# The opening norm of a two-layer decoder, computed on a transposed input

## The chip, the cores and the metric

The kernel runs on one core of a Trainium2 chip. The metric is device time in microseconds (us) for one call; smaller is better. Five engines with instruction streams of their own appear in the profile: PE (TensorE, matrix products), DVE (VectorE), ACT (ScalarE), POOL (GpSimd) and SP (SyncE, which here issues nearly all DMA transfers, one after the other in the order of its list).

## The reference

The input x has 1024 tokens of 1024 channels in float32. Two layers follow each other, each with a norm ahead of it; only the first norm and what reads its result, `h`, are touched here.

```python
def rmsnorm(x, g):
    y = x * lax.rsqrt(jnp.mean(x * x, axis=-1, keepdims=True) + NORM_EPS)
    return y * g
...
for i in range(2):                       # layer 0: FoX, layer 1: NSA
    h = rmsnorm(x, norm_g[i])
    x = x + mixer_i(h)                   # the mixer ends with (o * silu(z)) @ w_out
return rmsnorm(x, final_g)
...
def fox_mixer(h, w_in, b_f, w_out):      # layer 0
    q, k, v, f, z = split(h @ w_in)      # 16 heads of 64 channels; f: one gate per head
    c = cumsum(log_sigmoid(f + b_f), axis=tokens)
    logits = q k^T / 8 + c[query] - c[key]          # causal, softmax over the keys
    return (softmax(logits) @ v * silu(z)) @ w_out
```

The norm divides each token by the root of the mean square over its channels and multiplies each channel by a gain.

## The kernel before

TensorE contracts over the 128 partitions, so that every projection of h needs h transposed: channels on partitions, tokens along the free dimension. The names are `P` = 128 partitions, `KC` = 8 chunks of 128 channels, `NT` = 8 tiles of 128 tokens, and two *halves* of 512 tokens. h^T lies in `hT[half]` as two tiles, hi and lo (in the rows `hT0_0_0`, `hT0_0_1` for half 0, `hT0_1_0`, `hT0_1_1` for half 1; the profile calls all of them hT). hi is h rounded to the type fp32r and lo is what the rounding left, h - hi. A weight is split in the same way into `whi` and `wlo` (`load_w`: a 512 KB transfer into `wst`, a cast on DVE, a subtraction on POOL; `wst` has one buffer, `whi` and `wlo` two each). A projection is then three products per chunk, whi with hi, whi with lo, wlo with hi (`mm3`, L132 to L134), 24 products of 512 columns for one half.

**The opening** (`opening`) reads x in eight token tiles of 512 KB and, once, the gain spread over all partitions (`gB`, 512 KB). For each tile, `Norm` squares it on ACT and sums over the channels along the free dimension in the same instruction, ACT takes the root, DVE the reciprocal, and one DVE instruction of 1024 columns (L105) multiplies x by the token's factor and by gB. `to_hT` then transposes: eight products with `ident` into two PSUM tiles (L115), ACT casts them out of PSUM as hi (L119), DVE subtracts for lo (L120). As soon as the first four tiles are through, k_0 (the first half of the k projection of the first pair of heads, from `fox_k(0)`) and pf_0 (the projection to the forget gates, `forget_gate`) are interleaved with the transposes of the last four.

**What is behind it.** `fox_k` evicts each half of k into `KH` and `KL`, ACT and DVE alternating, and copies both across partitions with DMAs. `forget_gate` evicts its projection with two DVE instructions into `f2` and `fT` (L278, L279), passes fT through a DMA that changes its layout (`fg0`), does log-sigmoid and cumulative sum in some twenty short DVE and ACT instructions (L284 to L302), and sums over blocks with one plain float32 product on PE, `pc` (L305). The result goes to DRAM as `cD`, and comes back as the bias tiles `B` (16 transfers of 512 KB over the kernel) to which POOL adds the causal mask (`Bd`, L563). Then follow the projections v (`v_0`, `v_1` for its halves), z and q of the first pair of heads, k, v, q, z of the next ones as fillers between scores, and the attention of the first layer. A helper `wo_copy` writes the output weights back to DRAM in split form in the background (transfers of `wD`), on SP's queue too.

**What sets the order.** In the opening, the lists of PE, DVE and ACT stand in the order of the code (`tc.manual_schedule`); POOL's and SP's lists, and everything behind the opening, are ordered by a scheduler with a model of the costs, which is also free to move instructions that follow in the code. Each engine works its list strictly in order, so an instruction that waits holds up all that stand behind it.

## Time and profile before

| | |
|---|---|
| median of 3 runs | 1571.32 us (1570.53 to 1571.86) |
| profiled execution | 1573.4 us, of which the profile's span is 1571.6 us |
| mean granted TensorE clock in it | 0.98 |
| PE busy | 95% of the span |
| DVE, ACT, POOL busy | 71%, 56%, 35% |
| DMA | 213 MB moved, mean 136 GB/s |

The profile is one execution, and the times are in microseconds from the start of its span. A row of the timeline gives start, duration, engine, line, operation, out<-in and the shapes; in square brackets stands how long the engine was idle before it and what ended that. A row of the page's groups gives, for one line and operation, the count, the busy time and the mean duration in ns, and then the idle time before these instructions. A row of a table by stretches gives, for a window A:B, the busy time and the number of instructions on each engine (PE, its weight loads PEld, DVE, ACT, POOL), then the granted clock, the DMA engines' share and the rate in GB/s. The durations of matmuls are modelled by the profiler and overlap; what counts for them is the distance from start to start. A plain float32 product is two records.

### The profile page before, as it was taken

The numbers are of one execution on the slowest core, as the hardware profiler recorded it, in microseconds if no ns is written. First come the engines' busy times: TensorE is split into PE (matmuls) and PEld (weight loads), VectorE is DVE, ScalarE is ACT, GpSimd is POOL, SyncE is SP. The second block draws the span as 40 slices with busy tenths as digits, with TensorE's granted clock in tenths as the row PEclk, the third lists the DMA queues.
The fourth block names the chain that finished last, engine by engine and source line by source line (L and its number), as shares of the span: only waits on it lengthen the run. The fifth ranks groups of instructions, "written<-read, shape, count | busy, mean of one in ns | idle before, by whom it ended". The sixth has DMA issues, their size and how long they took to land.

```text
span 1571.6 us, 26098 instructions
## 1 busy us (share of the span) xinstructions
PE 1488.9 (95%) x8536; PEld 1245.3 (79%) x8536; DVE 1110.7 (71%) x2880; ACT 873.6 (56%) x2145; POOL 555.6 (35%) x596
## 2 busy tenths in 40 slices
PE   6999999999999787999999989999999999999898
PEld 4888888888777566878888777788888888888786
DVE  6568878788686855456464776888888888887433
ACT  5455655555555643233133544777787788787522
POOL 1222222232223400034242232546555556556400
PEclk9999999999999878999999999999999999999999
DMA  7777787777677756332436555502312312212452
GB/s 259 234 144 163 161 165 150 165 161 160 148 153 171 165 119 208 115 119 90 141 120 186 188 188 174 188 28 82 122 53 69 122 41 68 75 55 81 141 161 94
DMA packets 253945, 213.14 MB, mean 136 GB/s; under 512 B 179632, under 2 KB 201008, under 8 KB 253552
## 3 DMA queue, kind: packets, MB, share of 16 engines
q1 hardware_dynamic: 253808, 211.46, 49.2%
q8 instruction: 68, 1.11, 0.3%
q14 instruction: 69, 0.57, 0.1%
HBM read 123.06 MB, written 46.20 MB: 108 GB/s over the span
## 4 chain that ended last, share of the span: by engine, by line
PE 52%; DVE 12%; ACT 7%; DMA 4%; issue 4%; POOL 1%; SPq 0%; POOLq 0%; DVEq 0%; ACTq 0%
PE ptp_n L1250 7%; PE S_n L1226 7%; PE O_n L1259 3%; PE O_n L1258 3%; PE y L134 3%; PE y L133 3%; PE y L132 3%; ACT cP L1033 2%; DVE hl L594 2%; ACT P L592 1%; PE nz L132 1%; PE nz L133 1%; PE nz L134 1%; DMA wo<-wD 1%; ACT P_n L1234 1%
## 5 line engine op out<-in xcount | busy, mean ns | idle before, releaser
L1238 POOL TENSOR_SCALAR P_n<-P_n,l_n,gates 128x640 f32<-128x640 f32 (+7 forms) x256 | 200.9, 791 | 176.2 <-DVE l_n L1236 143.5
L145 DVE TENSOR_TENSOR ptl_n<-ptp_n,pth_n 128x512 fp32r<-128x512 f32 (+1 forms) x272 | 181.3, 672 | 35.3 <-ACT pth_n L144 31.6
L1234 ACT ACTIVATE P_n<-P_n,m_n 128x640 f32<-128x640 f32 (+7 forms) x256 | 188.5, 737 | 23.8 <-DVE m_n L1233 22.0
L144 ACT CAST pth_n<-ptp_n 128x512 fp32r<-128x512 f32 (+1 forms) x272 | 153.7, 568 | 73.5 <-PE ptp_n L1250 72.1
L592 ACT ACTIVATE P<-P,m 128x512 f32<-128x512 f32 (+1 forms) x192 | 116.8, 609 | 126.6 <-DVE m L583 125.9
L1226 PE MATMUL S_n<-nk,nq 128*128 128x320 f32 (+5 forms) x768 | 171.7, 333 | 0.2 <-DVE m_n L1233 0.2
L1250 PE MATMUL ptp_n<-ident,P_n 128*128 128x128 f32 x1056 | 166.9, 275 | 4.6 <-DVE ptl_n L145 2.9
L563 POOL TENSOR_TENSOR Bd<-B,tri 128x128 f32<-128x128 f32 x128 | 61.4, 491 | 250.6 <-DVE m L583 237.3
L1250 PEld LDWEIGHTS ptp_n<-ident,P_n 128*128 128x128 f32 x1056 | 124.6, 140 | 30.9 <-DVE ptl_n L145 8.1
L1258 PE MATMUL O_n<-pth_n,nv 128*128 128x512 f32 (+3 forms) x384 | 140.1, 369 | 0.8 <-DVE ot_n L1269 0.3
L1226 PEld LDWEIGHTS S_n<-nk,nq 128*128 128x128 f32 x768 | 128.0, 188 | 15.3 <-DVE m_n L1233 1.9
L594 DVE SCALAR_TENSOR_TENSOR hl<-P,hl 128x512 f16<-128x512 f32 (+1 forms) x192 | 125.7, 670 | 19.5 <-ACT hl L593 18.1
L1259 PE MATMUL O_n<-ptl_n,nv 128*128 128x512 f32 (+3 forms) x384 | 120.7, 338 | 0.1
L1233 DVE CUSTOM_DVE_ANT_0 P_n<-S_n,wmask 128x128 f32<-128x128 f32 (+1 forms) x192 | 113.3, 591 | 9.0 <-PE S_n L1226 4.7
L132 PE MATMUL y<-wo,ohi 128*128 128x512 f32 x240 | 97.1, 405 | 8.7 <-ACT ohi L688 4.6
L133 PE MATMUL y<-wo,ohi 128*128 128x512 f32 x240 | 96.6, 403 | 3.7 <-POOL wo L526 3.7
L134 PE MATMUL y<-wo,olo 128*128 128x512 f32 x240 | 95.8, 401 | 2.0 <-DVE olo L468 1.4
L593 ACT ACTIVATE hl<-P 128x512 f16<-128x512 f32 (+1 forms) x192 | 92.7, 513 | 3.4 <-DMA pT<-hl 1.7
L1258 PEld LDWEIGHTS O_n<-pth_n,nv 128*128 128x128 f32 x384 | 72.6, 189 | 6.9 <-DVE ot_n L1269 1.3
L574 PE MATMUL S<-KH,Q 128*128 128x512 f32 (+1 forms) x192 | 68.7, 372 | 8.0 <-DVE m L583 7.8
L1259 PEld LDWEIGHTS O_n<-ptl_n,nv 128*128 128x128 f32 x384 | 73.0, 190 | 2.2 <-DVE ptl_n L145 0.3
L608 PE MATMUL O<-v,pT 128*128 128x128 f16 x576 | 61.8, 226 | 8.3 <-DVE ot L620 4.7
(361 smaller groups left out, 4030.1 us busy)
## 6 DMA issues: line engine op xcount, KB each, us to landing
nq<-qD SPq DMA_DIRECT2D x64, 256.0 KB
B<-cD SPq DMA_DIRECT2D x16, 512.0 KB
wo<-wD SPq DMA_DIRECT2D x16, 512.0 KB
nq<-qD SPq DMA_DIRECT2D x64, 128.0 KB
of<-oF SPq DMA_DIRECT2D x12, 512.0 KB
x<-in_x_dram SPq DMA_DIRECT2D x8, 512.0 KB
wst_k<-in_fox_w_dram SPq DMA_DIRECT2D x8, 512.0 KB
wst_v<-in_fox_w_dram SPq DMA_DIRECT2D x8, 512.0 KB
```

What stands on the lines that cost most here:

```text
L132: T.matmul(ps, wh, mh, start=first, stop=False, **kw)
L133: T.matmul(ps, wh, ml, start=False, stop=False, **kw)
L134: T.matmul(ps, wl, mh, start=False, stop=last, **kw)
L144: A.copy(hi[:, 0:n], pt[:, 0:n])
L145: V.tensor_tensor(lo[:, 0:n], pt[:, 0:n], f(hi[:, 0:n]), OP.subtract)
L594: V.scalar_tensor_tensor(lo[:, cs], L[:, 0:n], UP, hi[:, cs], OP.mult, OP.subtract)
L1226: T.matmul(ps[:, b, 0:w], self.q[x][:, qi * P:(qi + 1) * P], k[:, k0 + b * w:k0 + b * w + w], start=(x == 0), stop=(x == 1))
L1234: A.activation(L, L, AF.Exp, bias=m, scale=-1.0, accum_out=lr[:, 0, qi:qi + 1])
L1238: G.tensor_scalar(L, L, lr[:, 1, qi:qi + 1], gates[:, i, x:x + 1], OP.mult, OP.mult)
L1250: T.transpose(pt[:, (x + i) * P:(x + i + 1) * P], L[:, kb * P - k0:(kb + 1) * P - k0], ident)
L1258: T.matmul(po[:, d], v, hi[:, c], start=(b == i == 0), stop=False)
L1259: T.matmul(po[:, d], v, lo[:, c], start=False, stop=(b == len(self.blocks) - 1 and i == len(pieces) - 1))
```

## The change

x is passed a second time in transposed layout, `xT`, and the gain as `norm_gT`, one column of 128 for each chunk. Only the opening of layer 0 uses them; x itself is still read later for the residual. In the opening, channels are now on partitions from the start:

- x^T is loaded in 16 pieces of 256 KB (128 channels by 512 tokens); gB is no longer loaded.
- ACT squares a piece into `sq` (two buffers), and PE sums over the channels: four plain float32 products per piece, each with 128 tokens of sq as the stationary side and a column of ones as the moving side, accumulating over the eight chunks in PSUM (`sum_0`, `sum_1`, one column per token tile).
- `factors(half)`: root on ACT, reciprocal on DVE, a DVE copy that repeats each token's factor along 128 columns (`rb`), and four plain float32 products of it with ident, which leave in PSUM a tile (`r_0`, `r_1`) with each token's factor on all partitions.
- `chunk(half, k, eng)`: one DVE instruction multiplies the piece by the gain and by that tile (L373), ACT casts the result to hi (L375), and lo is subtracted on DVE for even and on POOL for odd chunks (L376).
- The transposes and their evictions are gone. k_0 is interleaved with the chunks of half 0 and the sums of half 1, pf_0 and the second half of k with the chunks of half 1.

```diff
     def opening():
-        gB = st.tile([P, D], F32, name="gB")
-        xs = []
-        for t in range(NT):
-            xs.append(st.tile([P, D], F32, tag="x", bufs=7, name=f"x_{t}"))
-            dma(xs[t], a["x"][t * P:(t + 1) * P, :])
-            if t == 0:
-                dma(gB, a["norm_g"][0:1, :].to_broadcast([P, D]))
-            if t == 1:
-                wst = wp.tile([P, KC, P], F32, tag="wst", bufs=1, name="wst_k0")
-                dma(wst, a["fox_w"][8])
-            if t == 3:
-                dma(wfst, a["fox_w_f"].rearrange("(k p) c -> p k c", p=P))
-                dma(bf, a["fox_b_f"].rearrange("o h -> h o"))
-                dma(below, a["below"])
+        gT = st.tile([P, KC], F32, name="gT")
+        dma(gT, a["norm_gT"])
+        wst = wp.tile([P, KC, P], F32, tag="wst", bufs=1, name="wst_k0")
+        xs = [st.tile([P, KC, 512], F32, name=f"xT_{half}") for half in range(2)]
+
+        def load_x(half, ks):
+            for k in ks:
+                dma(xs[half][:, k, :], a["xT"][k * P:(k + 1) * P, half * 512:half * 512 + 512])
+
+        load_x(0, range(6))
+        dma(wst, a["fox_w"][8])
+        load_x(0, range(6, 8))
+        dma(wfst, a["fox_w_f"].rearrange("(k p) c -> p k c", p=P))
+        dma(bf, a["fox_b_f"].rearrange("o h -> h o"))
+        dma(below, a["below"])
+        load_x(1, range(8))
         dma(tri, a["tri"])
+        ones = st.tile([P, 1], F32, name="ones")
+        G.memset(ones, 1.0)
         whi = wp.tile([P, KC, P], F32R, tag="whi", bufs=2, name="whi_k0")
         wlo = wp.tile([P, KC, P], F32R, tag="wlo", bufs=2, name="wlo_k0")
-        side = []
-        hs = {}
+        sums = [ps_s(f"sum_{half}") for half in range(2)]
+        rs = [ps_s("r_0"), ps_t("r_1")]
+
+        def square(half, k):
+            sq = st.tile([P, 512], F32, tag="sq", bufs=2, name=f"sq_{half}_{k}")
+            A.activation(sq, xs[half][:, k, :], AF.Square)
+            for t in range(4):
+                T.matmul(sums[half][:, t:t + 1], sq[:, t * P:(t + 1) * P], ones, start=(k == t == 0), stop=(k == KC - 1 and t == 3))
+
+        def factors(half):
+            r = st.tile([P, 8], F32, name=f"rms_{half}")
+            A.activation(r[:, 0:4], sums[half][:, 0:4], AF.Sqrt, bias=eps, scale=1.0 / D)
+            V.reciprocal(r[:, 4:8], r[:, 0:4])
+            rb = st.tile([P, 4, P], F32, name=f"rb_{half}")
+            V.tensor_copy(rb, r[:, 4:8, None].to_broadcast([P, 4, P]))
+            for t in range(4):
+                T.matmul(rs[half][:, t * P:(t + 1) * P], rb[:, t, :], ident, start=(t == 0), stop=(t == 3))
+
+        def chunk(half, k, eng):
+            h = st.tile([P, 512], F32, tag="h", bufs=3, name=f"h_{half}_{k}")
+            V.scalar_tensor_tensor(h, xs[half][:, k, :], gT[:, k:k + 1], rs[half], OP.mult, OP.mult)
+            hi, lo = (hT[half][i][:, k, :] for i in range(2))
+            A.copy(hi, h)
+            eng.tensor_tensor(lo, h, f(hi), OP.subtract)
+
         with tc.manual_schedule(engines={T.engine, V.engine, A.engine}):
-            for t in range(NT + 1):
-                if t < NT:
-                    nm = Norm(st, xs[t], f"n0_{t}", 3)
-                    nm.square(slice(0, D))
-                    hs[t] = nm.finish(gB)
-                if t:
-                    to_hT(hs.pop(t - 1), t - 1, hT, f"n0_{t - 1}", (ps_s, ps_t))
-                if t == 1:
-                    V.tensor_copy(whi, wst)
-                    G.tensor_tensor(wlo, wst, f(whi), OP.subtract)
-                    wq.append((whi, wlo))
-                if t == 4:
-                    V.tensor_copy(wf[:, :, 0:H], wfst)
-                    V.tensor_tensor(wf[:, :, 32:32 + H], wfst, f(wf[:, :, 0:H]), OP.subtract)
-                    side = [k0] * 9 + [gate0] * 8
-                if t >= 5:
-                    for g in side[0:5]:
-                        next(g)
-                    del side[0:5]
-            for g in side:
-                next(g)
+            for k in range(KC):
+                square(0, k)
+            V.tensor_copy(whi, wst)
+            G.tensor_tensor(wlo, wst, f(whi), OP.subtract)
+            wq.append((whi, wlo))
+            factors(0)
+            for k in range(KC):
+                chunk(0, k, V if k % 2 == 0 else G)
+                square(1, k)
+                if k:
+                    next(k0)
+            V.tensor_copy(wf[:, :, 0:H], wfst)
+            V.tensor_tensor(wf[:, :, 32:32 + H], wfst, f(wf[:, :, 0:H]), OP.subtract)
+            factors(1)
+            next(k0)
+            next(k0)
+            side = [gate0] * 8 + [k0] * 8
+            for k in range(KC):
+                chunk(1, k, V if k % 2 == 0 else G)
+                for g in side[0:2]:
+                    next(g)
+                del side[0:2]
...
     r["x"] = np.ascontiguousarray(inputs["x"][0])
+    r["xT"] = np.ascontiguousarray(r["x"].T)
+    r["norm_gT"] = np.ascontiguousarray(inputs["norm_g"][0].reshape(KC, P).T)
```

Behind the opening the code is unchanged, but the scheduler's lists move. Three places show it. The first is PE's list around the first product of k_0. Before (transposes `pth`, the x4 of a row are four products):

```order
L115 MATMUL pth_n0_3_0_205<-ident_72,h_n0_3_180 128x128 x4
L115 MATMUL pth_n0_3_1_212<-ident_72,h_n0_3_180 128x128 x4
L115 MATMUL pth_n0_4_0_227<-ident_72,h_n0_4_200 128x128 x4
L115 MATMUL pth_n0_4_1_234<-ident_72,h_n0_4_200 128x128 x4
L132 MATMUL k0_0_245<-hT0_0_0_94,whi_k0_127 128x512
L133 MATMUL k0_0_245<-hT0_0_1_95,whi_k0_127 128x512
L134 MATMUL k0_0_245<-hT0_0_0_94,wlo_k0_128 128x512
L132 MATMUL k0_0_245<-hT0_0_0_94,whi_k0_127 128x512
```

Now (`sum_0`, `sum_1` are the sums of squares, `r_0` the spread factors):

```order
L360 MATMUL sum_0_133<-ones_129,sq_0_6_175 128x1 x4
L360 MATMUL sum_0_133<-ones_129,sq_0_7_181 128x1 x4
L369 MATMUL r_0_135<-ident_72,rb_0_192 128x128 x4
L360 MATMUL sum_1_134<-ones_129,sq_1_0_202 128x1 x4
L360 MATMUL sum_1_134<-ones_129,sq_1_1_212 128x1 x4
L132 MATMUL k0_0_222<-hT0_0_0_94,whi_k0_131 128x512
L133 MATMUL k0_0_222<-hT0_0_1_95,whi_k0_131 128x512
L134 MATMUL k0_0_222<-hT0_0_0_94,wlo_k0_132 128x512
L360 MATMUL sum_1_134<-ones_129,sq_1_2_230 128x1 x4
```

What moved: the transposes are gone, and ahead of k_0's first product now stand all sums of half 0, the factors and the sums of two pieces of half 1; one group of sums stands between each two chunks of k_0.

The second place is DVE's list in the second half, from the eviction of k_0 on. Before (`KL_0_0` and `KL_0_1` are evictions of k_0, `f2` and `fT` those of the gate's projection `pf_0`, the outputs hT0_1_1 the lo tiles of half 1):

```order
L324 TENSOR_TENSOR KL_0_0_243<-k0_0_245,KH_0_0_241 64x512
L324 TENSOR_TENSOR KL_0_1_244<-k0_0_245,KH_0_1_242 64x512
L101 RECIPROCAL st_n0_7_303<-st_n0_7_303 128x1
L105 SCALAR_TENSOR_TENSOR h_n0_7_304<-x_7_124,st_n0_7_303,gB_103 128x1024
L120 TENSOR_TENSOR hT0_1_1_97<-pth_n0_6_0_309,hT0_1_0_96 128x4x128
L120 TENSOR_TENSOR hT0_1_1_97<-pth_n0_6_1_316,hT0_1_0_96 128x4x128
L120 TENSOR_TENSOR hT0_1_1_97<-pth_n0_7_0_333,hT0_1_0_96 128x4x128
L120 TENSOR_TENSOR hT0_1_1_97<-pth_n0_7_1_340,hT0_1_0_96 128x4x128
L278 COPY f2_299<-pf_0_300 16x512
L279 SCALAR_TENSOR_TENSOR fT_298<-pf_0_300,bf_99,f2_299 16x512
```

Now:

```order
L324 TENSOR_TENSOR KL_0_0_220<-k0_0_222,KH_0_0_218 64x512
L324 TENSOR_TENSOR KL_0_1_221<-k0_0_222,KH_0_1_219 64x512
L373 SCALAR_TENSOR_TENSOR h_1_0_326<-xT_1_107,gT_103,r_1_136 128x512
L278 COPY f2_331<-pf_0_332 16x512
L376 TENSOR_TENSOR hT0_1_1_97<-h_1_0_326,hT0_1_0_96 128x512
L373 SCALAR_TENSOR_TENSOR h_1_1_337<-xT_1_107,gT_103,r_1_136 128x512
L373 SCALAR_TENSOR_TENSOR h_1_2_345<-xT_1_107,gT_103,r_1_136 128x512
L279 SCALAR_TENSOR_TENSOR fT_330<-pf_0_332,bf_99,f2_331 16x512
L376 TENSOR_TENSOR hT0_1_1_97<-h_1_2_345,hT0_1_0_96 128x512
L373 SCALAR_TENSOR_TENSOR h_1_3_353<-xT_1_107,gT_103,r_1_136 128x512
```

What moved: the eviction f2 of pf_0, which stood behind the last of the lo subtractions of the second half, now stands behind the first chunk's product h_1_0 and ahead of its lo subtraction, and fT ahead of the lo of the third chunk.

The third place is POOL's list in the opening (`wlo_k0`, `wlo_v0` are split weights, L128 and L382 the same subtraction). Before:

```order
L361 TENSOR_TENSOR wlo_k0_128<-wst_k0_109,whi_k0_127 128x1024
L128 TENSOR_TENSOR wlo_v0_434<-wst_v0_431,whi_v0_433 128x1024
L128 TENSOR_TENSOR wlo_q0_440<-wst_q0_437,whi_q0_439 128x1024
L128 TENSOR_TENSOR wlo_z0_527<-wst_z0_524,whi_z0_526 128x1024
L563 TENSOR_TENSOR Bd_0_0_0_1_607<-B_0_0_602,tri_74 128x128
```

Now:

```order
L382 TENSOR_TENSOR wlo_k0_132<-wst_k0_105,whi_k0_131 128x1024
L376 TENSOR_TENSOR hT0_0_1_95<-h_0_1_208,hT0_0_0_94 128x512
L376 TENSOR_TENSOR hT0_0_1_95<-h_0_3_239,hT0_0_0_94 128x512
L128 TENSOR_TENSOR wlo_v0_460<-wst_v0_457,whi_v0_459 128x1024
L376 TENSOR_TENSOR hT0_0_1_95<-h_0_5_265,hT0_0_0_94 128x512
L376 TENSOR_TENSOR hT0_0_1_95<-h_0_7_291,hT0_0_0_94 128x512
L376 TENSOR_TENSOR hT0_1_1_97<-h_1_1_337,hT0_1_0_96 128x512
L376 TENSOR_TENSOR hT0_1_1_97<-h_1_3_353,hT0_1_0_96 128x512
```

What moved: eight lo subtractions of 512 columns are new on POOL, and the subtraction for v's weight stands in the middle of the four of half 0. On DVE, likewise, the cast of z's weight (`whi_z0`) stood behind the forget gate's arithmetic and now stands behind its second instruction (L284, L293). From v_1 on, PE's two lists are the same up to the place of the single product pc. On SP's list, twelve of the wD copies now stand ahead of the second half's KH and KL transfers and of the gate's layout transfer.

## The prediction

> **What bounds the kernel now.** I read the page for the whole, a table by stretches for the opening, then the timeline of the first 75 us engine by engine, and last the groups of instructions for prices.
>
> ```profile
> PE 1488.9 (95%) x8536; PEld 1245.3 (79%) x8536; DVE 1110.7 (71%) x2880; ACT 873.6 (56%) x2145; POOL 555.6 (35%) x596
> core 0: us, PE busy (x) PEld busy (x) DVE busy (x) ACT busy (x) POOL busy (x), PEclk, DMA share, GB/s
> 0.00:23.70 23.70, 9.37 (x39) 7.78 (x40) 14.89 (x21) 14.55 (x29) 3.75 (x9) 1.00 0.89 321
> 23.70:39.00 15.30, 13.96 (x71) 11.36 (x70) 11.38 (x19) 8.00 (x16) 3.38 (x1) 1.00 0.49 169
> 39.00:60.00 21.00, 21.00 (x94) 17.25 (x94) 10.49 (x25) 6.91 (x12) 3.28 (x2) 1.00 0.85 280
> 60.00:100.00 40.00, 40.00 (x196) 33.08 (x195) 24.43 (x59) 18.40 (x40) 13.90 (x14) 1.00 0.54 143
> ```
>
> TensorE bounds all but the opening: from 39 to 100 us it never stops. So the change is worth the shift of one point on PE, behind which nothing is new. I take the start of v_1, the second half of the first v projection: from there PE runs the same list before and after, but for the one product pc. These rows fix the points before:
>
> ```profile
> 23.82 0.78 PE L132 MATMUL k<-hT,whi_k 128*128 128x512 f32 x1
> ...
> 31.02 0.40 PE L275 MATMUL pf<-hT,wf 128*128 128x512 f32 x1
> ...
> 52.61 0.39 PE L134 MATMUL v<-hT,wlo_v 128*128 128x512 f32 x1
> 52.83 0.39 PE L132 MATMUL v<-hT,whi_v 128*128 128x512 f32 x1
> ```
>
> The first projection, k_0, starts at 23.8 and has its last product finished at about 31.2; v_1 starts at 52.8. Warm, a 512-column product takes 0.2275 us of PE (start to start), so three are 0.68.
>
> **Price of a sum.** The sums are plain f32, and PE writes a plain f32 product as two records, each with a weight load. The only such product before is pc:
>
> ```profile
> 58.28 0.28 PE L305 MATMUL pc<-fg,below 128*128 128x1 f32 x2
> 58.42 0.48 PE L132 MATMUL q<-hT,whi_q 128*128 128x512 f32 x1
> 58.73 0.39 PE L133 MATMUL q<-hT,whi_q 128*128 128x512 f32 x1
> ...
> 22.20 1.97 PE L115 MATMUL pth_n<-ident,h_n 128*128 128x128 f32 x8 [0.98 <-DVE h_n L105]
> ...
> 28.06 1.03 PE L115 MATMUL pth_n<-ident,h_n 128*128 128x128 f32 x8
> ```
>
> From 58.28 to 58.73 stand both halves of pc and one 512-column product: 0.45 - 0.23 = 0.22, so 0.11 per record, though it streams one column: the load is what it pays for. A chunk (four tokens' tiles, two records each) is 8 x 0.115 = 0.92 us. That is with a fast PE. Eight transposes take 1.97 us at 22.2 and 1.03 at 28.1: early on PE runs at half speed, and a chunk is then about 1.8. When it gets fast is seen here:
>
> ```profile
> 25.25 0.48 PE L132 MATMUL k<-hT,whi_k 128*128 128x512 f32 x1
> 25.57 0.39 PE L133 MATMUL k<-hT,whi_k 128*128 128x512 f32 x1
> ...
> 22.05:25.46 3.41, 3.26 (x12) 2.97 (x13) 3.34 (x8) 2.97 (x6) 0.00 (x0) 1.00 0.00 0
> 568.20:571.60 3.40, 1.82 (x7) 0.89 (x6) 3.37 (x15) 2.23 (x6) 0.92 (x2) 1.00 0.50 96
> 571.60:575.00 3.40, 2.98 (x22) 2.43 (x22) 1.61 (x9) 2.05 (x7) 0.00 (x0) 0.50 0.31 63
> 581.80:585.20 3.40, 3.40 (x10) 2.63 (x9) 1.74 (x6) 0.71 (x2) 0.00 (x0) 0.50 0.43 84
> ```
>
> PE got fast at 25.4, after 3.2 us with almost no gap; at 568 to 571.6 it was busy for 1.82 of 3.40 us and slow afterwards; 2.98 of 3.40 did not bring it back, an unbroken stretch did. [...]
>
> **First half, k_0.** The first chunk lands about when x lands now (ACT's first Square starts at 4.58). Prices of the rest:
>
> ```profile
> L525 ACT CAST wo<-wo 128x512 fp32r<-128x512 f32 x32 | 18.2, 617 | 11.2 <-DMA wo<-wD 10.8
> L100 ACT ACTIVATE st_n<-st_n,eps 128x1 f32<-128x1 f32 x8 | 2.4, 294 | 0.3
> L632 DVE SCALAR_TENSOR_TENSOR z<-pto,vsc,z 128x512 f32<-128x512 f32 x16 | 12.0, 747 | 18.1 <-PE pto L630 17.9
> L901 DVE TENSOR_TENSOR rt_q<-rt_q,ru_q 128x512 f32<-128x512 f32 x4 | 2.6, 680 | 0.0
> L1275 POOL TENSOR_TENSOR no<-no,nz 128x512 f32<-128x512 f32 x16 | 21.1, 1320 | 4.1 <-DVE nz L82 3.3
> L324 DVE TENSOR_TENSOR KL<-k,KH 64x512 fp32r<-64x512 f32 x4 | 2.8, 688 | 2.6 <-ACT KH L323 2.5
> L323 ACT CAST KH<-k 64x512 fp32r<-64x512 f32 x4 | 2.3, 582 | 8.8 <-PE k L134 7.3 <-DVE KL L324 1.5
> ...
> 13.18 2.35 POOL L361 TENSOR_TENSOR wlo_k<-wst_k,whi_k 128x1024 fp32r<-128x1024 f32 x1 [11.19 <-DVE st_n L101]
> 13.21 3.40 DVE L105 SCALAR_TENSOR_TENSOR h_n<-x,st_n,gB 128x1024 f32<-128x1024 f32 x1
> ```
>
> - Sums of half 0: first Square done at 5.2; two chunks on a slow PE (3.6), six on a fast one (5.7), 0.2 to drain: 14.7. The loads hide below this: eight 256 KB pieces and the 512 KB weight at 1251.00's rate (last fence) land by about 11.
> - Factors: Sqrt 0.29, reciprocal 0.16, spreading copy between 0.35 and 0.68 (half a 1024-column weight cast at one end, a 512-column copy out of PSUM at the other; I take 0.5), eight records with 128 columns 1.0 and draining 0.25: 17.1 with hand-overs. Then h 0.75 and its cast 0.62: 18.5.
> - Sums 0 and 1 of half 1 stand ahead of k_0's first product on PE; their Square comes behind that cast (19.1). PE has been three quarters idle since 15 and is slow: 3.6 more. k_0 starts at 22.7, no earlier than now by more than a microsecond.
> - The loop then has two limits of the same size. PE: 0.92 + 0.68 + 0.09 for a weight load with nothing over it = 1.7 per chunk. DVE with POOL: the 1024-column product of DVE at 13.21 took 3.40 us where its equals take 1.28, exactly because POOL subtracts until 15.53; both have two inputs in SBUF. The odd chunks' subtractions on POOL therefore shut out the even ones' on DVE: h 0.72, cast 0.62, POOL 1.33, DVE 0.62 and hand-overs 0.1 in a row make 3.4 per two chunks, 1.7 per chunk. Eight chunks: 13.6. Half a slow product at the start and POOL's wlo_v (2.35), now in the middle of the loop between DVE's cast and its next subtraction, add 1 to 2.5, taken as 1.6. k_0 finishes at 37.9 against 31.2: 6.7 late. Bounds: 34 if PE is fast throughout and wlo_v hides; 41.
>
> **Second half, to v_1.** KH, KL, KH, KL alternate on ACT and DVE: 2.7. h_0 0.7. Then DVE's list has f2, which waits for the sixteen pf products (3.7, end at 37.9 + 3.9 = 41.8); f2 0.68, subtraction 0.65: 43.1. Three pairs at 3.4: 53.3. The last chunk, h 0.65, cast 0.65, POOL 1.35: 56.0. Its five products 1.15 and the 17 of v_0 that stand behind them 3.9: v_1 starts at 61.1, 23.2 after k_0. Before it was 21.6 (31.2 to 52.8), transposes included. So 1.6 more, bounds -1.5 (no shutting out: three pairs at 2.3) and +2.5. PE fills the waits with seven products of v_0, no more.
>
> **Behind v_1.** DVE's cast whi_z now stands ahead of the forget gate's arithmetic, and it waits for the last product that reads whi_v:
>
> ```profile
> 58.30 0.69 DVE L127 CAST whi_z<-wst_z 128x1024 fp32r<-128x1024 f32 x1 [0.26 <-PE v L133]
> ...
> 71.39 1.72 POOL L563 TENSOR_TENSOR Bd<-B,tri 128x128 f32<-128x128 f32 x4 [9.87 <-DMA B<-cD]
> 1251.00:1251.50 0.50, 0.50 (x5) 0.45 (x4) 0.44 (x2) 0.44 (x2) 0.00 (x0) 1.00 0.90 320
> ```
>
> The gate's chain behind it takes 5 us (table load 1.28, Ln and some twelve short DVE instructions), PE reaches pc 4.3 us after v_1's end: 0.7 of waiting. The bias B, which now comes just as the first scores do (71.39 against 71.0), comes some 3 us late; PE has 75 products of z and k before the next scores, so I cost it at 0 to 2.8, taking 0.5. Removed and costing nothing: gB's 512 KB, the PSUM evictions, 64 transposes (13 us of PE busy time, all of it in waits for DVE). On SP, twelve of the wD copies now go ahead of the second KH and of fg's load; at 1.4 us each they are through by 54, fg comes at 60. If they are not, fg adds to those 2.8.
>
> **Sum.** 6.7 + 1.6 + 0.7 + 0.5 = 9.5 us later. The profiled execution took 1573.4 (span 1571.6), 2.1 above the median of 1571.3; so 1582.9 in a profile like it, 1580.8 as the median.
>
> **Rivals.**
> - *PE stays slow through the sums.* If only streamed columns make PE fast, one-column products never do. Half 0: 5.2 + 8 x 1.8 = 19.6; factors on a slow PE 3.8, h and cast 1.4: 24.8; then eight times (1.8 + 1.43), the second spreading 2: 53. Plus 23.2: 76, and with the tail +24.5: 1596. Against it: at 22.05 to 25.46 1.97 us were transposes, and PE still came up, while 2.98 us of mostly long products at 571.6 did not suffice: occupied time seems to count. [...] Chance 0.22.
> - *DVE and POOL don't shut each other out, or sums are nearly free.* Without the first, half 2 saves 3.2 and half 1 about 1: +5.3, 1576.6; with both, k_0 at 31 to 32 and 1572. The 3.40 us row is against it. Chance 0.1.
> - *Given back behind (not slower).* From 540 to 630 us PE is busy for 72 of 90 us. If a wait there ended on a transfer that does not depend on the opening, 9 us would vanish: 1571 to 1573. It decides if the oF and pT transfers there start at the same time as before; they carry products of the first layer, which come late. Chance 0.1.
>
> [...] Here slow transposes take 0.25 each, fast ones 0.13; no one-column product on a slow PE is shown.
>
> **Chances.** My case 0.58 (own range 1577 to 1586), the rivals 0.22, 0.1, 0.1. The range to hold 8 in 10: 1573 (low prices) to 1597 (slow PE). A change under 0.2% (3.1 us) can't be told from none: faster 0.04, same 0.11 (given back, lowest prices), slower 0.85.
>
> **What would show it.** First k product near 22.7, last near 37.9; sum chunks at 1.8 and then 0.92; subtractions on POOL at 1.3 and DVE's with a mean well over 0.68; v_1 at about 61; the rest shifted alike. I am wrong if k_0 ends by 31 (sums or exclusion overpriced) or after 50 (slow PE).

## The result, and the profile after

The changed kernel takes 1594.45 us (median of 4 runs, 1593.84 to 1596.46) against 1571.59 (1570.53 to 1572.40) for the kernel before on the same chip: a ratio of 1.0148 [1.0131, 1.0166], 22.9 us slower. The sign was forecast; the size, 9.5 us, was less than half of it. The time lies within the range given, but at the place of the rival in which PE stays slow through the sums (1596). The profiled execution took 1596.46 us, 2.0 above its median, as the profiled execution of before was 1.8 above this one.

The page of after, its first line, and the table by stretches over the first three stretches shown for before:

```profile
PE 1516.3 (95%) x8616; PEld 1271.5 (80%) x8616; DVE 1107.8 (69%) x2876; ACT 873.4 (55%) x2139; POOL 566.2 (36%) x605
0.00:23.70 23.70, 15.86 (x72) 15.51 (x72) 2.05 (x4) 7.41 (x13) 3.80 (x10) 1.00 0.87 299
23.70:39.00 15.30, 14.55 (x56) 13.31 (x56) 9.06 (x14) 7.91 (x15) 7.50 (x5) 1.00 0.30 106
39.00:60.00 21.00, 19.01 (x67) 15.38 (x67) 7.62 (x12) 3.91 (x7) 1.99 (x2) 0.97 0.44 150
```

PE's share is still 95% and its busy time has *grown* by 27 us, though 64 transposes are gone. It is now PE that is busy from 5 us on, and DVE, busy for 14.89 of the first 23.7 us before, is nearly idle (2.05). The granted clock reads 1.00 in the first two rows; nothing in this column says that PE is slow, and the last section tells why. The timeline of PE says it:

```profile
5.32 13.79 PE L360 MATMUL sum<-ones,sq 128*128 128x1 f32 x64 [5.32 <-ACT sq L358]
20.19 2.08 PE L369 MATMUL r<-ident,rb 128*128 128x128 f32 x8 [1.09 <-DVE rb L367]
...
28.05 0.77 PE L132 MATMUL k<-hT,whi_k 128*128 128x512 f32 x1
28.62 0.63 PE L133 MATMUL k<-hT,whi_k 128*128 128x512 f32 x1
29.05 0.63 PE L134 MATMUL k<-hT,wlo_k 128*128 128x512 f32 x1
29.48 1.70 PE L360 MATMUL sum<-ones,sq 128*128 128x1 f32 x8
31.04 0.78 PE L132 MATMUL k<-hT,whi_k 128*128 128x512 f32 x1
...
44.41 1.70 PE L360 MATMUL sum<-ones,sq 128*128 128x1 f32 x8
...
47.40 1.91 PE L369 MATMUL r<-ident,rb 128*128 128x128 f32 x8
...
51.66 0.56 PE L276 MATMUL pf<-hT,wf 128*128 128x512 f32 x1
52.06 0.39 PE L275 MATMUL pf<-hT,wf 128*128 128x512 f32 x1
...
73.83 0.39 PE L132 MATMUL v<-hT,whi_v 128*128 128x512 f32 x1
84.98 0.38 PE L305 MATMUL pc<-fg,below 128*128 128x1 f32 x2 [1.47 <-DVE fg L301]
93.74 0.48 PE L602 MATMUL S<-KH,Q 128*128 128x512 f32 x1
```

The first row holds all sums of half 0: 64 records without a gap in 13.79 us, 0.215 each, and not one of the eight groups gets shorter. ACT, which has two sq buffers, waits for PE instead (idle 1.07 ahead of each Square from the third on). In the loop a chunk takes 2.99 us (28.05 to 31.04): 1.56 for its sums and 1.43 for three long products, the last two 0.43 apart, where on a fast PE they are 0.23 apart. PE is busy without a gap from 28 to 50 and remains at this speed (0.43 between long products). The last sums end at 45.97. Then come three long products (of 512 columns), the spreading of half 1 and only long products, and PE gets fast at 52: the pf products are 0.23 apart from there. It is slow once more (0.43) from 58.8 to 62.3, around three waits of 0.91, 0.46 and 0.63 us for chunks of half 1. k_0 ends at about 50.6, v_1 starts 21.0 us later than before, the first score product S 22.7 later, and the span ends 23.1 later. Nothing is given back behind the opening.

### The profile page after: what moved, and what is told of

Its sections match the earlier page's. It is cut to its first block, busy times and chain, and to the rows that moved or that the text cites. A ratio compares the mean times of both kernels' runs of the same rounds, so it can differ in the third digit from the quotient of the medians.

```text
span 1594.7 us, 26274 instructions
## 1 busy us (share of the span) xinstructions
PE 1516.3 (95%) x8616; PEld 1271.5 (80%) x8616; DVE 1107.8 (69%) x2876; ACT 873.4 (55%) x2139; POOL 566.2 (36%) x605
## 4 chain that ended last, share of the span: by engine, by line
PE 68%; DVE 14%; ACT 7%; issue 4%; DMA 4%; POOL 1%; SPq 0%; POOLq 0%; DVEq 0%; ACTq 0%
PE ptp_n L1278 6%; PE S_n L1254 6%; PE O_n L1287 3%; PE y L134 3%; PE y L133 3%; PE O_n L1286 3%; PE y L132 3%; DVE hl L622 2%; PE k L132 2%; PE k L133 2%; PE v L132 2%; PE k L134 2%; PE v L133 2%; PE v L134 2%; ACT P L620 2%
## 5 line engine op out<-in xcount | busy, mean ns | idle before, releaser
L1262 ACT ACTIVATE P_n<-P_n,m_n 128x640 f32<-128x640 f32 (+7 forms) x256 | 188.5, 738 | 25.4 <-DVE m_n L1261 23.7
L636 PEld LDWEIGHTS <-pT 128*128 128x128 f16 x576 | 50.8, 100 | 22.8 <-issue 15.4
```

The source lines that it names most:

```text
L1262: A.activation(L, L, AF.Exp, bias=m, scale=-1.0, accum_out=lr[:, 0, qi:qi + 1])
```

## The experiments

Each expectation has a theory A and a theory B of its own. Theory A of e1, e2 and e7 is that only streamed columns make PE fast, so that one-column products never do. The times below are from the start of each profiled span. Three points on PE's list for every kernel, and the median with its ratio to before:

| kernel | last k_0 product | v_1 | first S | median us | ratio to before |
|---|---|---|---|---|---|
| before | 30.79 | 52.83 | 71.00 | | |
| after | 49.96 | 73.83 | 93.74 | 1594.45 | 1.0148 [1.0131, 1.0166] |
| e1_stream | 39.02 | 61.64 | 81.61 | 1584.76 | 1.0083 [1.0065, 1.0101] |
| e2_block | 46.41 | 69.26 | 91.60 | 1595.90 | 1.0150 [1.0134, 1.0165] |
| e3_lo_dve | 50.02 | 71.03 | 91.36 | 1595.50 | 1.0147 [1.0132, 1.0162] |
| e4_acc | 40.85 | 61.40 | 83.58 | 1584.43 | 1.0077 [1.0060, 1.0094] |
| e6_f32r | 38.68 | 58.67 | 79.14 | 1579.63 | 1.0051 [1.0035, 1.0066] |
| e7_feed | 36.10 | 56.06 | 76.53 | 1579.48 | 1.0043 [1.0030, 1.0056] |
| e9_pc | 50.16 | 72.80 | 90.70 | 1591.54 | 1.0123 [1.0108, 1.0138] |
| e8_order | 34.90 | 55.59 | 75.43 | 1577.65 | 1.0027 [1.0016, 1.0038] |
| e10_psum | 32.99 | 52.12 | 73.77 | 1573.53 | 1.0008 [0.9993, 1.0024] |
| e11_gate | 32.97 | * | 72.10 | 1573.13 | 0.9999 [0.9988, 1.0010] |
| e12_gate2 | 32.16 | * | 69.67 | 1572.63 | 1.0000 [0.9989, 1.0012] |
| e13_gate3 | 31.72 | * | 65.90 | 1567.70 | 0.9958 [0.9944, 0.9971] |

(* v_1 is interleaved with other work there. Each ratio is to the runs of before on the same chip, whose medians were 1571.6 to 1573.5.) From S to the end of the span there remain 1496.8 to 1501.4 us in all of them. So the opening decides, but a difference of up to 4.6 us between two kernels can also arise behind it.

### Is it the columns? e1_stream

The same squares, still plain f32, become the moving side: 512 streamed columns against a stationary block of ones.

```diff
-            for t in range(4):
-                T.matmul(sums[half][:, t:t + 1], sq[:, t * P:(t + 1) * P], ones, ...)
+            T.matmul(sums[half], ones, sq, start=(k == 0), stop=(k == KC - 1))
```

The sums come out along the free dimension; eight tiny records bring the roots back onto partitions.

> Sums by one plain float32 product per piece in which the squares are the moving side (512 columns, ones as 128x128 stationary side), the same kind of product and on a slow PE about the same PE time per piece (1.7 us) as the four one-column products; the row of sums is then turned back into a column by four small products, 1 to 2 us more per half. Theory A (only streamed columns make PE fast, one-column products leave it slow): the first two to four pieces take 1.7 us each, then 0.9; sums of half 0 done at 14 to 16 us instead of 19.1, first k product at 22 to 24 instead of 28.05, last at about 37 to 40 instead of 50, whole time 1581 to 1585 against 1594.5. Theory B (plain float32 products never make PE fast, or PE is slow here for another reason, such as the time since the start): 1.7 us per piece throughout, first k product at 29 to 30, last at about 51, time 1595 to 1597.

The timeline of PE in e1_stream:

```profile
5.37 9.82 PE L359 MATMUL sum<-sq,ones 128*128 128x512 f32 x16 [5.37 <-ACT sq L358]
...
24.11 1.41 PE L132 MATMUL k<-hT,whi_k 128*128 128x512 f32 x1
...
26.08 1.02 PE L359 MATMUL sum<-sq,ones 128*128 128x512 f32 x2
...
27.64 1.02 PE L359 MATMUL sum<-sq,ones 128*128 128x512 f32 x2
...
39.02 0.40 PE L134 MATMUL k<-hT,wlo_k 128*128 128x512 f32 x1
```

PE gets fast within the sums of half 0, whose 16 records take 9.82 us, and which are done at 15.2 instead of 19.1; the spreading behind them takes 1.16, where after needed 2.08. It falls slow again behind the factors (the four records from 20.99 take 3.12, 0.78 each), and is fast from the second chunk of k_0 on. In the loop a chunk takes 1.56 us (26.08 to 27.64); three fast products take 0.69 of them, which leaves 0.87 for the two records, near the 0.92 at which the prediction had priced the one-column ones. k_0's last product comes 10.9 us earlier and the median is 9.7 us lower. All of it is as theory A had it, the first k product 0.1 us later. It also agrees with the sum of the main case, whose premise was a fast PE: k_0 ends at 39.4 (forecast 37.9), and the kernel is 12.4 us slower than before on its chip (forecast 9.5).

### Long products alone: e2_block

The sums of half 1 all go ahead of k_0, so that its 24 products stand together.

```diff
             for k in range(KC):
                 chunk(0, k, ...)
                 square(1, k)
-                if k:
-                    next(k0)
...
+            for k in range(KC):
+                next(k0)
```

> As the changed kernel, but all sums of half 1 stand ahead of k_0's first product on PE instead of between its chunks; the number of products is the same. Theory A (the one-column products between the chunks keep PE slow): the sums still take 1.7 us per group, the first k product comes at 36 to 38 us, and then 24 products without sums between them get fast after 3.4 to 7 us, so that k_0 ends at about 45 to 46 instead of 50.6 and the whole time falls by 4 to 6 us to about 1589. Theory B (PE is slow until about 52 us whatever stands between the products): k products 0.43 us apart to the end, k_0 ends at 47 to 48, PE fast no earlier than 51, time about 1592.

The timeline of PE in e2_block, at k_0 and behind the wait at pc:

```profile
39.32 0.77 PE L132 MATMUL k<-hT,whi_k 128*128 128x512 f32 x1
...
42.45 0.63 PE L133 MATMUL k<-hT,whi_k 128*128 128x512 f32 x1
...
43.23 0.40 PE L132 MATMUL k<-hT,whi_k 128*128 128x512 f32 x1
...
79.67 0.38 PE L305 MATMUL pc<-fg,below 128*128 128x1 f32 x2 [2.08 <-DVE fg L301]
...
80.70 0.63 PE L132 MATMUL q<-hT,whi_q 128*128 128x512 f32 x1
```

PE gets fast in the middle of k_0, 3.9 us behind its first product (0.43 apart up to 42.88, 0.23 from 43.23 on); behind the sums ahead of it, 10.4 us of one-column products in one unbroken row (0.217 each), it was still slow. The last k_0 product comes 3.6 us earlier, much as theory A expected. The total was a miss: v_1 came 4.6 earlier, S only 2.1. PE waited longer at pc (2.08 us against 1.47) and fell slow again behind it (0.43 apart from 80.70 to 83.69). The median did not move by more than its uncertainty, where theory A had 4 to 6 us.

### The shutting out of DVE and POOL: e3_lo_dve

All subtractions for lo go to DVE, each one chunk behind its h.

```diff
-            eng.tensor_tensor(lo, h, f(hi), OP.subtract)
+            return lambda: V.tensor_tensor(lo, h, f(hi), OP.subtract)
...
+                nxt = chunk(half, k + 1, V) if k < KC - 1 else None
+                lo()
+                lo = nxt
```

> As the changed kernel, but all lo subtractions are on DVE, each behind the next chunk's product h. First half bounded by PE's sums, so k_0 ends at 50 to 51 as before. Theory A (a POOL subtraction shuts out the DVE subtraction with both inputs in SBUF): the stretch from k_0's end to v_1 shrinks from 23.2 to about 20.5 us, DVE's subtractions have a mean of 0.65 instead of about 1.0, time about 1592. Theory B (POOL takes work off DVE, no exclusion): the stretch stays at 23 or grows by up to 2 us, time 1594 to 1597.

The groups by line, DVE's and POOL's subtractions, first in after, then in e3_lo_dve:

```profile
L376 DVE TENSOR_TENSOR hT<-h,hT 128x512 fp32r<-128x512 f32 x8 | 7.7, 968 | 6.5 <-ACT hT L375 6.5
L376 POOL TENSOR_TENSOR hT<-h,hT 128x512 fp32r<-128x512 f32 x8 | 10.6, 1326 | 41.0 <-ACT hT L375 41.0
```

```profile
L376 DVE TENSOR_TENSOR hT<-h,hT 128x512 fp32r<-128x512 f32 x16 | 11.6, 722 | 3.1 <-ACT hT L375 3.1
```

With POOL's share taken over, DVE's subtractions get *shorter*, from a mean of 968 ns to 722. From k_0's end to v_1 pass 20.4 us instead of 23.2, as expected; how much of that is the shorter subtractions and how much the other order on DVE's list, the run doesn't separate. In the loop of half 0 nothing is gained, since there PE is the limit. The median did not show the 2.4 us by which S came earlier; its uncertainty is as large.

### Fewer sums on PE: e4_acc

DVE adds up the squares of the eight pieces, and PE sums once per half. lo as in e3.

```diff
+            V.tensor_tensor(acc[half], acc[half], sq, OP.add)
...
+        def total(half):
+            for t in range(4):
+                T.matmul(sums[half][:, t:t + 1], acc[half][:, t * P:(t + 1) * P], ones, ...)
```

> The squares are added up over the chunks on DVE (seven additions of 512 columns per half), so that PE does four one-column products per half instead of 32; lo on DVE as in the run beside it; the weight k is loaded behind all pieces of half 0 and its lo subtracted on DVE. Theory A (what the change lost is the 128 slow records of sums and the slow k products between them): r_0 is there at about 15 to 16 us, first k product at 17.5 to 19, the first half is then bounded by DVE (h, lo and an addition, 2.0 us per chunk), k_0 ends at 32 to 35, v_1 starts at 52 to 56 against 73.8 and 52.8 before the change; time 1571 to 1575. Theory B (the loss is in the order of half 2 or behind v_1, not in the sums): at most 10 us of the 23 come back, time 1584 or more.

The timeline of PE in e4_acc, and its row in the table by stretches:

```profile
30.01 0.79 PE L133 MATMUL k<-hT,whi_k 128*128 128x512 f32 x1 [2.42 <-DVE hT L383]
...
35.74 1.87 PE L367 MATMUL sum<-ones,acc 128*128 128x1 f32 x8 [2.65 <-DVE acc L363]
20.00:41.00 21.00, 13.79 (x32) 8.65 (x33) 16.21 (x26) 7.93 (x15) 2.84 (x1) 1.00 0.71 266
```

A miss: k_0 starts at 20.2, 3.6 us earlier than before, but its last product comes at 40.85 and not by 35. PE is busy for 13.8 of 21 us and waits for DVE, which now adds, multiplies and subtracts for every chunk (16.2 of 21 us), once 2.42 while POOL's wlo_v holds up DVE's subtraction (2.18 us, the others 0.68), and 2.65 for the last sum of half 1. With these gaps PE stays slow too (0.43 between products up to 40.2). The load moved from PE to DVE, and half of the loss is back. The time, 1584.43, is what theory B had (1584 or more), but not for its reason: v_1 comes 12.4 us earlier than in after.

### Sums in fp32r, and a PE kept busy: e6_f32r, e7_feed

e6 streams the squares as in e1, but rounded to fp32r (one record instead of two), with lo on DVE, the weight of k behind all pieces of half 0, and the factors of half 1 ahead of k_0's last chunk. e7 is e6 with 34 products of a zero weight, whose result is overwritten, put ahead of and among the sums of half 0.

```diff
-            sq = st.tile([P, 512], F32, ...)
+            sq = st.tile([P, 512], F32R, ...)
...
+        def feed(n):            # only in e7: feed(12) first, feed(2) behind each piece, feed(6)
+            for i in range(n):
+                T.matmul(rs[1], wf[:, 0, :], wf[:, 0:4, :], start=True, stop=True)
```

> Sums as in e1_stream, but with the squares rounded to fp32r (one product of 512 columns per piece, 0.23 to 0.43 us of PE instead of 0.9 to 1.7); all lo subtractions on DVE one chunk behind h, as in e3_lo_dve; the weight k behind all pieces of half 0, its lo on DVE; factors of half 1 ahead of k_0's last chunk, and the first two h of half 1 ahead of k_0's eviction. Theory A (what the change lost is the slow one-column products on PE and then the sharing of DVE with POOL; the transposed opening by itself needs less of PE and DVE than the one before): r_0 at 16 to 18 us, first k product at 18 to 20, last at 29 to 32, v_1 at 46 to 50 against 52.8 before the change, first scores at 65 to 70 against 71.0, time 1565 to 1571. Theory B (the transposed opening is slower in itself, by its factors and DVE's two passes over h): v_1 at 55 or later, time over 1574.

> As e6_f32r, with 34 more products of 512 columns on PE whose operands are zeros and whose result is overwritten, from about 2 us until r_0: they do nothing but keep PE streaming. Theory A (streaming alone makes PE fast): dummy products 0.43 us apart at first, 0.23 from 5 to 9 us on; the small products that turn the sums into a column take 0.11 instead of 0.21 us per record and the spreading 1.0 instead of 2.0 us, r_0 comes 1 to 2 us earlier than in e6_f32r and v_1 0 to 2 us earlier. Theory B (PE is slow early for another reason, or zeros do not count): no product under 0.4 us before 15 us, and the added products only delay.

The timeline of PE in e6_f32r, then in e7_feed:

```profile
13.83 1.86 PE L367 MATMUL r<-one,row 1*128 1x1 f32 x8 [0.83 <-ACT row L365]
16.43 2.08 PE L372 MATMUL r<-ident,rb 128*128 128x128 f32 x8 [0.74 <-DVE rb L370]
```

```profile
2.05 5.49 PE L364 MATMUL r<-wf 128*128 128x512 f32 x12 [2.05 <-POOL wf L266]
...
8.40 0.40 PE L360 MATMUL sum<-sq,ones 128*128 128x512 f32 x1
...
13.78 1.05 PE L371 MATMUL r<-one,row 1*128 1x1 f32 x8 [0.36 <-ACT row L369]
15.57 1.16 PE L376 MATMUL r<-ident,rb 128*128 128x128 f32 x8 [0.74 <-DVE rb L374]
```

With streamed columns of zeros PE gets fast as well: it is so from about 8 us on, after 6 us of them (0.43 from product to product at 7.33, 0.23 at 8.40), and the tiny records and the spreading then cost 1.05 and 1.16 instead of 1.86 and 2.08. So in these runs the slow PE of the first 25 us is no matter of elapsed time, but of what PE has been given to do. v_1 comes 2.6 us earlier in e7 than in e6, though PE falls slow twice more, from about 21.8 and from about 32 us (0.43 apart from 21.93 to 24.91 and from 35.67 to 38.66); the medians are equal within their uncertainty. By its numbers e6 is theory B's case (v_1 at 58.67 and 1579.63 us, where theory A had 46 to 50 and 1565 to 1571). That the transposed opening is slower in itself does not follow: e10 below brings v_1 ahead of before's with another order. What is left in e6 is DVE, which stands idle for 4.54 and 1.57 us around the factors of half 1: its reciprocal waits for the tiny records, which stand behind seven chunks of k_0 on PE's list.

### The wait at pc: e9_pc

The kernel after, with pc reading a zero instead of the gate's last scan: the sums over blocks are left out of the cumulative sum.

```diff
-        T.matmul(pt[:, 0:1], below, r[:, 3:4], start=True, stop=True)
+        T.matmul(pt[:, 0:1], below, zero, start=True, stop=True)
```

> As the changed kernel, but the product pc reads a constant column of zeros instead of the forget gate's block sums (that part of the cumulative sum is left out), so that PE does not wait for DVE there. Theory A (of the 23 us, 1.5 to 1.8 lie behind v_1, in PE's wait at pc, as DVE's cast whi_z delays the gate's arithmetic): from v_1 to the first scores 18.2 to 18.6 us instead of 19.9, time 1.3 to 1.8 us shorter. Theory B (the first scores wait for the bias B or for q anyway): still 19.5 to 20, no difference.

PE's list now has pc at 54 us, ahead of v_1, and no wait there. From v_1 to S pass 17.9 us instead of 19.9, a little more than theory A expected, and the median is 2.9 lower (1591.54 against 1594.45; the intervals of the two ratios still touch). So the gate's chain on DVE, which stands behind the cast whi_z, costs the changed kernel about 2 us, where the prediction had 0.7 and 0.5 for the bias behind it.

### Can the change be repaired? e8_order, e10_psum, e11_gate, e12_gate2, e13_gate3

All are e7 with another order. e8 squares six pieces of half 1 ahead of k_0, takes the factors of half 1 behind the fourth chunk of k_0, and interleaves pf_0 with it. e10 also splits `factors` in two, so that DVE need not wait in the middle, spreads the squares of half 1 over the first chunks of half 0, and gives pf_0 another PSUM tile.

```diff
 # e8 against e7
+            for k in range(6):
+                square(1, k)
+                feed(1)
...
+                if k == 3:
+                    factors(1)
 # e10 against e8
-            pt = ps_a(f"pf_{half}")
+            pt = (ps_a if half else ps_s)(f"pf_{half}")
...
+                if k == 3:
+                    column(1)
+                if k == 4:
+                    spread(1)
```

> As e7_feed (sums streamed in fp32r, PE kept streaming until r_0, lo on DVE), with another order: squares and sums of half 1 right behind the factors of half 0, so that the factors of half 1 are there before DVE is through with half 0; pf_0 interleaved with k_0 and pf_1 with the second half of k. In e6_f32r DVE stood idle for 4.5 and 1.6 us around the factors of half 1 and ACT and PE had idle time from 14 to 19 us. Theory A (e6_f32r and e7_feed were held by this order, not by what the transposed opening needs): DVE works without a gap over 1 us from the first h at about 17 to the last lo at about 43, v_1 at 46 to 49 us against 56.1 and 52.8 before the change, first scores at 65 to 69 against 71.0, time 1565 to 1570. Theory B (the wait at pc and the gate's chain, not the opening, set the first scores): v_1 early, but PE's wait at pc grows by as much, first scores at 71 to 76, time 1571 or more.

> As e8_order, with its three gaps mended: pf_0 is accumulated in a PSUM tile of the scores' pool, so that pf_1 needs no tile that DVE has yet to clear (PE stood still for 4 us there, and was slow for 3 more); the squares of half 1 are spread over the first three chunks of half 0 instead of ahead of them (ACT's casts, and so DVE, waited 2.2 us); the reciprocal of half 1 stands one chunk later on DVE than the root on ACT (DVE waited 2.5 us). Theory A (these gaps held e8_order): DVE's last lo at 43 to 45 us instead of 48.6, v_1 at 48 to 51 instead of 55.6, first scores at 68 to 71 against 71.0 before the change, time 1569 to 1573. Theory B (DVE is full anyway, or other waits take their place): v_1 at 53 or later, time 1574 or more.

e8 missed what was expected of it: v_1 comes at 55.6, not at 46 to 49. k_0 is through by 35.3, but then PE stops for DVE's subtraction and falls slow (0.43 apart from 40.80 on), as its timeline shows; below it the timeline of e10_psum at pc and its table by stretches:

```profile
40.06 0.51 PE L133 MATMUL k<-hT,whi_k 128*128 128x512 f32 x1 [2.88 <-DVE hT L383]
40.40 0.60 PE L134 MATMUL k<-hT,wlo_k 128*128 128x512 f32 x1
```

```profile
62.50 0.38 PE L305 MATMUL pc<-fg,below 128*128 128x1 f32 x2 [1.61 <-DVE fg L301]
59.00:62.50 3.50, 1.90 (x9) 1.24 (x7) 2.24 (x12) 2.35 (x5) 1.83 (x1) 1.00 0.56 215
64.00:67.00 3.00, 3.00 (x8) 2.33 (x8) 0.42 (x3) 0.51 (x1) 0.00 (x0) 0.50 0.88 151
```

In e10 v_1 starts at 52.1, 0.7 earlier than before: the opening's loss is gone. But PE is half idle ahead of pc and slow from 64 to 67 (8 products in 3 us), and S comes 2.8 us later than before. Both are a little later than theory A had them (48 to 51, and 68 to 71). The time ties with before, since 3.8 us less remain behind S. e11 and e12 then put nine steps of q ahead of the gate's remainder; e11 also gives pf_1 a tile of the scores' pool and spreads the factors of half 1 one chunk later, and e12 starts the gate's chain directly behind the opening.

```diff
 # e11 against e10
+            q0 = fox_q(0, next_w()) if p == 0 else ()
             if p == 0:
+                for _ in range(9):
+                    yield next(q0)
                 yield from gate0
...
 # e12 against e11
             chunks(1, then)
+            next(gate0)
+            next(gate0)
+            next(k0)
+            next(gate0)
```

> As e10_psum, with pf_1 too in the scores' PSUM pool (so that v_0 has a tile from the start of half 2 and fills PE's waits for DVE), wf and the spreading of half 1 one chunk later (DVE waited 1.3 and 1.4 us there), and pc behind the first half of q in the order of the code, so that PE need not wait for the gate there. Theory A: all of v_0 stands between the products of half 2, v_1 ends at 50 to 52 us instead of 57.6, no wait over 0.5 us at pc, first scores at 64 to 70 us against 73.8 in e10_psum and 71.0 before the change, time 1565 to 1571. Theory B (the gate's chain to the bias B sets the first softmax): first scores earlier, but DVE's first score instruction (72.3 before the change) waits for B or Bd to 72 or later, time 1571 to 1574.

> As e11_gate, with the eviction of pf_1 (f2, fT) ahead of that of k on DVE, and the gate's arithmetic at a place in the order of the code right behind. Theory A (the gate's chain is late in e11_gate): fg is loaded 1.4 us earlier, B and Bd land up to 1.5 us earlier, time 0 to 2 us under e11_gate. Theory B (the chain is not what the first softmax waits for, or v's scaling, which now stands ahead of it on DVE, gives it back): within 1 us of e11_gate.

e11 missed theory A: PE waits 3.15 us at pc, S comes at 72.10 and not by 70, and the time ties with before. e12 is within 0.5 us of e11, as its theory B had it. The row of pc in e11_gate, then the timelines of PE and DVE in e12_gate2:

```profile
66.52 0.38 PE L305 MATMUL pc<-fg,below 128*128 128x1 f32 x2 [3.15 <-DVE fg L301]
```

```profile
53.56 0.39 PE L132 MATMUL q<-hT,whi_q 128*128 128x512 f32 x1
66.60 0.38 PE L305 MATMUL pc<-fg,below 128*128 128x1 f32 x2 [3.13 <-DVE fg L301]
69.67 0.47 PE L646 MATMUL S<-KH,Q 128*128 128x512 f32 x1
49.49 0.74 DVE L279 SCALAR_TENSOR_TENSOR fT<-pf,bf,f 16x512 f32<-16x512 f32 x1
56.58 0.69 DVE L127 CAST whi_z<-wst_z 128x1024 fp32r<-128x1024 f32 x1 [4.41 <-DMA wst_z<-in_fox_w_dram]
60.27 0.28 DVE L284 SCALAR_TENSOR_TENSOR fg<-fg 128x128 f32<-128x128 f32 x1
77.22 0.56 DVE L655 CUSTOM_DVE_ANT_0 P<-S,B 128x384 f32<-128x384 f32 x1 [6.28 <-DMA B<-cD]
```

The first q product comes 4.9 us earlier than in before (58.42), but PE then waits 3.13 us at pc, S is only 1.3 earlier, and DVE's first softmax instruction, which waits for the bias B, comes 4.9 *later* than before's 72.31. The gate's input fT is ready at 50.2; its first instruction on DVE runs at 60.3, behind a wait for z's weight and the scaling of v. e13 shortens just this: ACT issues the layout transfer, and z's weight is cast behind the gate's arithmetic.

```diff
 # e13 against e12
-        dma(x, fT)
+        nc.scalar.dma_start(x, fT)
+        yield 0
...
+            wq.append(wsec(*fox_order.pop(0)))       # v's weight
             chunks(1, then)
+            wq.append(wsec(*fox_order.pop(0)))       # q's
+            next(gate0)
             next(gate0)
             next(gate0)
             next(k0)
             next(gate0)
+            wq.append(wsec(*fox_order.pop(0)))       # z's, behind the gate
```

> The forget gate's chain alone is shortened against e12_gate2: its layout transfer is issued by ACT as soon as fT is there (in e12 it stood on SP's list behind four other transfers, 50.2 to 53.5 us), and DVE's gate instructions stand ahead of the cast whi_z and of v's scaling (in e12 the first came at 60.3, behind a wait of 4.4 us for z's weight). Theory A, the gate's chain was the bound in e12: first gate instruction near 53, pc at 59.5 to 61 with a wait of at most 1 us (e12: 66.6 and 3.1), first score product S at 66 to 67.5 (69.7), DVE's first softmax row at 70.5 to 73 (77.2), and the time 2 to 4 us below before: 1568 to 1571 against about 1572.9, ratio 0.9975 to 0.9990. Theory B, another chain takes its place (the scaling of v and the eviction of q, now later on DVE, or z's weight): pc comes early, but S not before 69, and the time ties with before, 1571.5 to 1574.

The same rows of e13_gate3:

```profile
59.32 0.28 PE L306 MATMUL pc<-fg,below 128*128 128x1 f32 x2
65.90 0.48 PE L651 MATMUL S<-KH,Q 128*128 128x512 f32 x1
53.26 0.29 DVE L285 SCALAR_TENSOR_TENSOR fg<-fg 128x128 f32<-128x128 f32 x1
70.53 0.56 DVE L660 CUSTOM_DVE_ANT_0 P<-S,B 128x384 f32<-128x384 f32 x1 [2.16 <-DMA B<-cD]
```

The gate starts 7 us earlier, PE no longer waits at pc, S is 5.1 and the first softmax row 1.8 us earlier than in before. The median is 1567.70 against 1573.46: 0.9958 [0.9944, 0.9971], about 5.8 us faster than before, more than theory A expected (2 to 4). This is the version that beats both kernels. The issue by ACT, the gate's place on DVE's list and the places of the weights changed together and were not tried one by one, and whether the kernel before would gain from the gate's earlier transfer by itself was not tried either.

## Why the prediction was right or wrong

**The step that failed** is "with a fast PE", used for the price of a sum after two slow chunks: sums of half 0 two slow groups and six fast, and in the loop 0.92 + 0.68 + 0.09 per chunk. PE never got fast while there were sums on its list (0.215 us per record and 0.43 per long product up to 45.97). Point by point, from the timeline of after:

- Sums of half 0 done at 14.7: 19.1, so 4.4 later. The rival had 19.6.
- From there to the first k product 8.0: measured 8.95, chiefly since the spreading took 2.08 (a slow PE) where 1.0 was put.
- The loop 15.2 (22.7 to 37.9): 22.5 (28.05 to 50.6), 7.3 more; 2.99 per chunk, where 1.7 was put and the rival had 1.8 + 1.43 = 3.2. Together 12.7 us, which is nearly the whole of the 13.4 that the forecast lacks.
- Why the premise was chosen wrongly: the row "22.05:25.46 3.41, 3.26" was read as "occupied time counts". It holds 1.6 us of transposes (from 22.20) and 1.6 of 512-column products (from 23.82). The long products would hardly have done it alone: in after a stretch of the same length, from 31.54 on, holds 1.85 us of them, the rest sums, and PE stays slow (0.43). So in before the transposes, with 128 columns each, seem to have counted for something, and the error was to pass from them to sums that stream a single column. That the transposes counted is inferred from these two stretches; no run tries them alone. For the sums it is shown: e1 has the same squares of the same data type, but streamed, and e2 the same sums, but not between the long products.
- k_0's end to v_1, 23.2: measured 23.2 (50.6 to 73.83). That it fits so closely is partly luck: f2 came 4.45 us behind k_0's end and not 3.9, as the first pf products were slow (0.43 apart up to 51.66), while two chunks took 3.2 us (DVE's subtractions at 58.45, 61.66, 64.87) and not 3.4. POOL's subtractions do lengthen DVE's (1.21 at 58.45, 0.68 alone), and e3, without them and with another order on DVE's list, needs 20.4. So the second rival's first half is refuted.
- Behind v_1, 0.7 + 0.5: S comes 1.7 later than v_1's shift explains, 1.47 of it as the wait at pc. B was not late for DVE (first softmax row 1.31 after S in both kernels).
- Given back behind: no. From S to the end 1500.6 before, 1501.0 after.

With long products of streamed columns PE was fast 3.9 us behind the first of them in e2 and 6 us in e7. For one-column products 13.8 us without a gap were not enough in after, nor were the 18 us of sums and long products in turn (28.05 to 45.97), so that occupied time alone did not decide it there. The rival in which one-column products never make PE fast was the better guide; of the transposes themselves, before's rows rather say that they count for something, as told above.

## What to carry to other kernels

A reduction moved to PE as one-column products cost a weight load for each of its records here (0.215 us a record in after), and PE, which wasn't fast yet, stayed slow through them, so that the long products between them took 0.43 us instead of 0.23: cost such work at the slow price until long products have stood without it for some 3 to 6 us (an estimate from 2.9 in e3, 3.9 in e2 and 6.0 in after), or swap the operands so that the data stream, as in e1 (half 0 summed at 15.2 instead of 19.1). Read PE's speed from the distance between equal products, not from its busy share or the clock column. And when an opening has been shortened, look which chain ends last behind it: here the gate's, and only its earlier transfer and its place on DVE's list, together with the weights', turned the tie into a gain.

## What the runs showed of the hardware

- Records that stream one column (their weight loads are busy nearly as long as they are, 15.51 against 15.86 us in the first row of after's table) took twice as long on a slow PE too: 0.215 us each in after, against 0.11 for the two of pc on a fast one in before. The same eight tiny records show it in e6 and e7 (1.86 and 1.05 us for the eight).
- The granted clock reads 1.00 through the whole slow opening of after because the trace has no record of the clock there: its first record begins at 52.02 us, when PE gets fast, and the column gives 1.00 where there is none. From 58.84 to 62.26 us, where PE is slow again, the column reads 0.50. So it does in the slow stretch of e10 (64 to 67 us), with the same 0.43 us from product to product.
- A wait's length alone did not tell whether PE was slow behind it. Behind the 3.15 us at pc in e11 the products are 0.43 apart (67.38 to 69.94), behind the 3.13 in e12 0.23; behind the 1.61 in e10 they are 0.43 apart from 64.12 on, behind the 2.04 in e7 0.23. What decides it is not shown.
- Two h products of DVE, each with one operand in PSUM, take 1.40 us together in after beside POOL's wlo_v (31.15), and 1.40 with nothing on POOL beside them (24.34). DVE's subtraction with two operands in SBUF takes 1.21 beside POOL's (58.45) and 0.67 without (55.66). POOL's wlo_v, which runs beside such a subtraction at its start, took 2.83. But POOL's own subtraction of 512 columns took 1.27 beside DVE's (57.83) as well as without (38.45).

```profile
30.64 2.83 POOL L128 TENSOR_TENSOR wlo_v<-wst_v,whi_v 128x1024 fp32r<-128x1024 f32 x1
31.15 1.40 DVE L373 SCALAR_TENSOR_TENSOR h<-xT,gT,r 128x512 f32<-128x512 f32 x2
58.45 1.21 DVE L376 TENSOR_TENSOR hT<-h,hT 128x512 fp32r<-128x512 f32 x1
```

These rows of DVE and POOL in after show it; the last is a subtraction beside POOL's, and POOL's wlo_k, of the same shape as this wlo_v, took 2.36 without DVE's beside it.
